# Down's blocks by block products in place of full-width products, and half of the weight sums by transfers

## The chip, the core and the metric

The kernel runs on one core of a Trainium2 chip. The metric is the device time of one execution in microseconds; a kernel's time is the median of its runs. All numbers of a profile come from one further execution, recorded by the hardware profiler.

## What is computed

The reference is one block of a diffusion transformer on 512 tokens of width 2048: a conditioning vector gives shifts, scales and gates, a token mixer of two branches is followed by a gated residual, and then comes the feed-forward part that this change is about, with an inner width D_FF of 5632:

```python
mod = jax.nn.silu(c) @ w_ada[layer] + b_ada[layer]
sh1, sc1, g1, sh2, sc2, g2 = jnp.split(mod[:, None, :], 6, axis=-1)
...
def swiglu(h, wg, wu, wd):
    return (jax.nn.silu(h @ wg) * (h @ wu)) @ wd
...
y, yc = token_mix(h, hc, p, need_ctx)
x = x + g1 * rmsnorm(y, norm_mix_post[layer])
h = modulate(x, norm_ffn_pre[layer], sh2, sc2)
x = x + g2 * rmsnorm(swiglu(h, w_gate[layer], w_up[layer], w_down[layer]), norm_ffn_post[layer])
```

Everything is float32. The kernel splits each operand into a high and a low part (hi, lo) that TensorE takes, and forms each product by three matmuls: hi x hi, hi x lo and lo x hi.

## The kernel before

Tokens stand on the free axis, features on the partitions, so that D_FF is 44 blocks of 128 rows and the width of 2048 is 16 blocks. A weight piece is 128 x 1024 numbers (512 KB, eight blocks of 128 x 128). SyncE's queue loads it (`raw`, or `rq` in the quads), ScalarE casts it to `whi`, VectorE subtracts to get `wlo`, and TensorE runs 24 matmuls on it. Both tiles have three buffers, so that weights are prepared some three pieces ahead of TensorE.

The feed-forward part has these stages:

- `gate_up` makes the first six of the 44 blocks of gate and up by halves of 256 tokens. `sums_of_x` meanwhile forms the sums of activation blocks that the next stage needs (`th`, `tl`; the plain blocks are `fh`, `fl`).
- `quad` treats the 38 remaining blocks as 19 pairs, for `w_gate` and then `w_up`: 38 quads. A quad is a product of 2 x 2 blocks of weights (two output blocks, two halves of the depth) with 2 x 2 blocks of activations (two halves of the depth, two halves of the tokens), formed by seven products of blocks instead of eight. Each product is one weight piece, 24 matmuls of 256 columns (`acc` in PSUM). Four weight pieces r11, r12, r21, r22 are loaded, and the sums of them that the seven products need are formed in place by four VectorE additions of 128 x 1024 (`rq<-rq,rq`). `early` and `end` combine the products into `R` on VectorE; gate times up goes to `hd` in DRAM.
- Down: `act_load` brings `hd` back (512 KB each), splits it, and `down_piece` runs ten chunks of four of the 44 blocks, at the full 512 columns, with sums kept in `y2`. Between its pieces come steps of the conditioning vector's product (`ada(1)`: a weight load and two VectorE operations of 128 x 512 each), the last of which give the final gate.
- The last chunk runs by two halves of 256 tokens (`down`), so that `last_done` and `finish` can normalise the first half, add the residual `x1d` and store while TensorE works on the second.

The order of each engine's instructions is set by a scheduler from the order of the code and by the buffers of each pool; `feed` and `push` put weights ahead of their matmuls.

## Time and profile before

| what | us |
|---|---|
| median of three runs | 2559.17 |
| lowest, highest | 2533.26, 2560.54 |
| the profiled execution, its time | 2562.26 |
| its span (first to last instruction) | 2560.4 |
| TensorE busy | 2436.5 (95%) |
| VectorE busy | 1802.5 (70%) |
| ScalarE busy | 914.5 (36%) |
| GpSimd busy | 458.5 (18%) |

PE is TensorE, PEld its weight load, DVE VectorE, ACT ScalarE, POOL GpSimd, SP SyncE, whose queue (SPq) issues the transfers. Matmuls overlap, so a matmul's duration (0.28 us at 256 columns) is longer than the distance to the next one; how fast TensorE goes is read from starts, or from the count in a window. "Idle before" is the time an engine stood still ahead of an instruction, with what ended it. Clock 1.00 is the full TensorE clock.

### The profile page before, as it was taken

What the parts mean: (1) busy time and instruction counts of PE and PEld (TensorE: products, weight loads), DVE (VectorE), ACT (ScalarE), POOL (GpSimd) and SP (SyncE); (2) the same over time, 40 slices, a digit from 0 to 9 for tenths busy, and PEclk for the clock granted to TensorE, in tenths of its full rate; (3) what the DMA queues carried; (4) which work ended last, traced back from release to release, by engine and by line L of the source; (5) the groups of instructions that cost most, each with busy time, mean ns of one, the idle gap of its engine ahead of it and who ended that gap; (6) DMA issues with size and microseconds to landing.
All of it is one profiled execution on the core that took longest, in us unless ns stands there. A gap on an engine that the chain in (4) does not pass through costs nothing.

```text
span 2560.4 us, 37510 instructions
## 1 busy us (share of the span) xinstructions
PE 2436.5 (95%) x14932; PEld 2118.2 (83%) x14932; DVE 1802.5 (70%) x2278; ACT 914.5 (36%) x1273; POOL 458.5 (18%) x421
## 2 busy tenths in 40 slices
PE   8999999899899999998999999999999899999996
PEld 3467879677667788998999999999999788888885
DVE  7986756788878867688877788878887763242234
ACT  3143325222223312355444444444444332231133
POOL 1230010566524244752000000000000000000004
PEclk9999999999899999999999999999999899999998
DMA  8867754435355565545633333333333484242233
GB/s 288 315 217 236 245 163 157 160 131 170 124 201 188 202 251 179 206 155 195 217 110 124 124 125 108 124 125 123 116 121 119 145 296 147 99 146 93 99 107 120
DMA packets 151223, 420.39 MB, mean 164 GB/s; under 512 B 15391, under 2 KB 46047, under 8 KB 149512
## 3 DMA queue, kind: packets, MB, share of 16 engines
q1 hardware_dynamic: 151048, 418.00, 48.0%
q8 instruction: 117, 1.92, 0.3%
q14 instruction: 58, 0.48, 0.1%
HBM read 382.82 MB, written 35.13 MB: 163 GB/s over the span
## 4 chain that ended last, share of the span: by engine, by line
PE 51%; DVE 2%; issue 1%; POOL 1%; DMA 1%; ACT 1%; POOLq 0%; SPq 0%; ACTq 0%; DVEq 0%
PE acc L83 22%; PE acc L1361 10%; PE acc L1360 10%; PE acc L1362 10%; POOL gs L80 1%; DVE wlo L80 1%; DMA x<-x1d 0%; DVE y2a L80 0%; ACT whi L170 0%; POOL y2a L80 0%; PE aux L83 0%; DMA raw<-in_w_down 0%; POOL yTa L80 0%; DMA st<-hd 0%; POOL r L80 0%
## 5 line engine op out<-in xcount | busy, mean ns | idle before, releaser
L80 DVE TENSOR_TENSOR wlo<-raw,whi 128x1024 fp32r<-128x1024 f32 x268 | 342.4, 1278 | 347.0 <-ACT whi L170 340.3
L170 ACT CAST whi<-raw 128x1024 fp32r<-128x1024 f32 (+1 forms) x284 | 293.2, 1033 | 740.1 <-PE acc L83 548.2
L80 DVE TENSOR_TENSOR wlo<-rq,whi 128x1024 fp32r<-128x1024 f32 x266 | 323.8, 1223 | 122.7 <-ACT whi L1321 117.9
L1321 ACT CAST whi<-rq 128x1024 fp32r<-128x1024 f32 x266 | 279.0, 1049 | 358.8 <-PE acc L1361 318.6
L1360 PE MATMUL acc<-th,whi 128*128 128x256 f32 x1216 | 341.7, 281 | 0.0
L1361 PE MATMUL acc<-tl,whi 128*128 128x256 f32 x1216 | 341.7, 281 | 0.0
L1362 PE MATMUL acc<-th,wlo 128*128 128x256 f32 x1216 | 341.7, 281 | 0.0
L80 POOL TENSOR_TENSOR gs<-gs,sq 128x256 f32<-128x256 f32 x91 | 84.8, 935 | 1386.4 <-ACT sq L74 1382.9
L83 PE MATMUL acc<-hh,whi 128*128 128x512 f32 x688 | 284.4, 415 | 4.4 <-ACT hh L74 4.2
L83 PE MATMUL acc<-hl,whi 128*128 128x512 f32 x688 | 276.8, 402 | 2.8 <-DVE hl L77 2.8
L83 PE MATMUL acc<-ah,whi 128*128 128x512 f32 (+1 forms) x688 | 264.0, 384 | 12.5 <-ACT ah L187 12.5
L83 PE MATMUL acc<-hh,wlo 128*128 128x512 f32 x688 | 275.9, 401 | 0.0
L83 PE MATMUL acc<-al,whi 128*128 128x512 f32 (+1 forms) x688 | 263.4, 383 | 0.0
L83 PE MATMUL acc<-ah,wlo 128*128 128x512 f32 (+1 forms) x688 | 263.3, 383 | 0.0
L1360 PE MATMUL acc<-fh,whi 128*128 128x256 f32 x912 | 256.3, 281 | 0.0
L1361 PE MATMUL acc<-fl,whi 128*128 128x256 f32 x912 | 256.3, 281 | 0.0
L1362 PE MATMUL acc<-fh,wlo 128*128 128x256 f32 x912 | 256.3, 281 | 0.0
L77 DVE SCALAR_TENSOR_TENSOR ada<-raw,cc,ada 128x512 f32<-128x512 f32 x240 | 202.8, 845 | 54.0 <-DMA raw<-in_ada 51.1
L1360 PEld LDWEIGHTS acc<-th,whi 128*128 128x128 f32 x1216 | 233.5, 192 | 0.0
L1361 PEld LDWEIGHTS acc<-tl,whi 128*128 128x128 f32 x1216 | 228.2, 188 | 0.0
L1362 PEld LDWEIGHTS acc<-th,wlo 128*128 128x128 f32 x1216 | 228.2, 188 | 0.0
L80 DVE TENSOR_TENSOR rq<-rq,rq 128x1024 f32<-128x1024 f32 x152 | 185.6, 1221 | 2.1
(325 smaller groups left out, 5001.6 us busy)
## 6 DMA issues: line engine op xcount, KB each, us to landing
raw<-in_ada SPq DMA_DIRECT2D x128, 512.0 KB, 3.9
raw<-in_w_down SPq DMA_DIRECT2D x88, 512.0 KB, 3.2
rq<-in_w_gate SPq DMA_DIRECT2D x76, 512.0 KB, 3.8
rq<-in_w_up SPq DMA_DIRECT2D x76, 512.0 KB, 3.4
ada<-in_ada SPq DMA_DIRECT2D x64, 512.0 KB, 4.9
raw<-in_w_hy SPq DMA_DIRECT2D x44, 512.0 KB, 4.0
raw<-in_w_out SPq DMA_DIRECT2D x41, 512.0 KB, 4.2
raw<-in_w_xbc SPq DMA_DIRECT2D x38, 512.0 KB, 3.8
```

The lines of the kernel that those rows point to most:

```text
L77: nc.vector.scalar_tensor_tensor(out=o, in0=a, scalar=s, in1=b, op0=op0, op1=op1)
L80: e.tensor_tensor(out=o, in0=a, in1=b, op=op)
L83: nc.tensor.matmul(o, lhsT, rhs, start=start, stop=stop)
L170: nc.scalar.copy(out=hi[:, :n], in_=raw[:, :n])
L1321: nc.scalar.copy(out=hi, in_=raw)
L1360: nc.tensor.matmul(p, wh, xh, start=k == 0, stop=False, skip_group_check=True)
L1361: nc.tensor.matmul(p, wh, xl, start=False, stop=False, skip_group_check=True)
L1362: nc.tensor.matmul(p, wl, xh, start=False, stop=k == 7, skip_group_check=True)
```

## The change

Sixteen of the 22 pairs of blocks of `hd` (pairs 3 to 18) now go through down by block products too: 16 more quads, in two chunks (c) of eight pairs, eight quads (m) each, on weights `w_ds`. Their activations are the results of the gate and up quads: `sums` forms the sums T when an up quad ends, and `hd` holds for each pair four result blocks and four sums. They take the place of the old activation operands in the same tiles: `replace` hangs 56 loads of 128 KB (`op_load`) and 56 splits (`op_split`: a ScalarE cast and a VectorE subtraction of 128 x 256) per chunk on the steps of the stream, around the quad at which the tile's old content has been used. Results of a down quad go to `y2d` in DRAM; at the end the first chunk's are loaded and the second chunk's added by accumulating transfers.

In every quad the sums of weights are formed in another way: a transfer issued by GpSimd adds the block of weights in DRAM to the piece in SBUF (`load_s1` for r21, and another into r11 after its first product); two additions remain on VectorE. The order of the seven products differs with it. Every third quad's first matmul is split at column 160. The steps `ada(1)` stand in the gate and up quads.

The six pairs left over (twelve blocks, `CP`) run in down by halves of 256 tokens, on weights `w_dc`, which are loaded once for each half; `kept` and `wload_big`, which kept weights for the second half, go.

```diff
-    hd = dram.tile([44, 128, 512], F32, name="hd")
+    hd = dram.tile([22, 128, 8, 256], F32, name="hd")
...
+    CP = [0, 1, 2, 19, 20, 21]
+    KICK = 160
...
+    def op_load(dst, src):
+        nc.sync.dma_start(dst[1].bitcast(F32), src)
+
+    def op_split(dst):
+        split(dst[0], dst[1], dst[1].bitcast(F32))
+
+    def replace(q, c, area):
+
+        for j in range(1, 7):
+            n = 7 * (q - 1) + j
+            for k in range(8):
+                d = place(j, k, 0)
+                at(n + 4, lambda d=d, k=k, j=j: op_load(d, hd[CH[c][k]][:, SRC[j], :]))
+                at(n + 6 + k // 4, lambda d=d: op_split(d))
+        for k in range(8):
+            d = place(0, k, area)
+            at(7 * (q - 4) + k, lambda d=d, k=k: op_load(d, hd[CH[c][k]][:, 0, :]))
+            at(7 * (q - 4) + k + 2, lambda d=d: op_split(d))
...
+    def load_s1(q):
+        r = qload("raw", quads[q][0][1, 0])
+        nc.gpsimd.dma_start(r, quads[q][0][1, 1], accum_op=ADD)
+        return r
...
-                    nc.tensor.matmul(p, wh, xh, start=k == 0, stop=False, skip_group_check=True)
+
+                    for c0, c1 in ((0, KICK), (KICK, 256)) if i == k == 0 and q % 3 == 0 else ((0, 256),):
+                        nc.tensor.matmul(p[:, c0:c1], wh, xh[:, c0:c1], start=k == 0 and c0 == 0, stop=False,
+                                         skip_group_check=True)
...
+                nc.sync.dma_start(hd[m][:, 0:4, :], R)
+                if m not in CP:
+                    sums(m, R)
+            else:
+                act(R[:, 1, :], R[:, 1, :], AF.Copy, scale=-1.0)
+                nc.sync.dma_start(y2d[kind, m], R)
+
+        def sums(m, R):
+            T = gu.tile([128, 4, 256], F32, tag="T", name=nm("T"))
+            tt(nc.vector, T[:, 0:4:2, :], R[:, 1:4:2, :], R[:, 0:2, :], SUB)
+            tt(nc.vector, T[:, 1, :], R[:, 3, :], T[:, 0, :], SUB)
+            tt(nc.vector, T[:, 3, :], T[:, 1, :], R[:, 2, :], SUB)
+            nc.sync.dma_start(hd[m][:, 4:8, :], T)
...
         feed(r11, body(0))
         feed(r12, body(1))
-        tt(nc.vector, r11, r11, r21, ADD)
-        feed(r11, body(2))
-        tt(nc.vector, r21, r21, r22, ADD)
+        feed(r22, body(2))
+        nc.gpsimd.dma_start(r11, src[1, 0], accum_op=ADD)
         feed(r21, body(3))
-        if nxt:
-            nxt.append(qload("ra", I[nxt[1]][2 * nxt[0], 0]))
-        tt(nc.vector, r11, r11, r22, ADD)
+        if more:
+            nxt["r11"] = qload("ra", quads[q + 1][0][0, 0])
         feed(r11, body(4))
-        if nxt:
-            nxt.append(qload("ra", I[nxt[1]][2 * nxt[0], 1]))
+        if more:
+            nxt["r21"] = load_s1(q + 1)
+        tt(nc.vector, r22, r22, r11, ADD)
         feed(r22, body(5))
-        tt(nc.vector, r11, r11, r12, ADD)
-        feed(r11, body(6))
...
+        if more:
+            nxt["r12"] = qload("ra", quads[q + 1][0][0, 1])
+        tt(nc.vector, r12, r12, r22, ADD)
+        if q < NG:
+            ada(1)
+        feed(r12, body(6))
+
+    replace(NG, 0, 256)
+    replace(NG + 8, 1, 0)
...
+    y2t = [gu.tile([128, 4, 256], F32, tag=f"th{m}", name=f"y2{m}") for m in range(8)]
+    for m in range(8):
+        nc.sync.dma_start(y2t[m], y2d[0, m])
+        nc.gpsimd.dma_start(y2t[m], y2d[1, m], accum_op=ADD)
...
+    def down(q, i, h, ps, done):
+        def run(w):
+            for u in range(8):
+                s, k = divmod(i * 8 + u, 12)
+                if k == 0:
+                    ps[s] = acc()[:, 0:256]
...
     for h in range(2):
         done = last_done(h)
         for q in range(8):
-            if not h and q > 2:
-                kept[q] = wload_big(I["w_down"][NCHUNK - 1, q], q - 3)
-            kept[q] = down(NCHUNK - 1, q, h * 256, h * 256 + 256, done, kept[q])
+            ps = {}
+            for i in range(3):
+                down(q, i, h, ps, done)
```

On VectorE in the middle of the gate and up quads, the sequence of one quad before (`rq` are weight pieces: r11 is rq_14985, r12 rq_15017, r21 rq_15078, r22 rq_15080):

```order
L80 TENSOR_TENSOR wlo_15083<-rq_14985,whi_15082 128x1024
L80 TENSOR_TENSOR R_14853<-R_14853,acc_14992 128x2x256
L80 TENSOR_TENSOR rq_14985<-rq_14985,rq_15078 128x1024
L80 TENSOR_TENSOR wlo_15118<-rq_15017,whi_15117 128x1024
L80 TENSOR_TENSOR R_14853<-R_14853,acc_14931 128x256
L80 TENSOR_TENSOR rq_15078<-rq_15078,rq_15080 128x1024
L80 TENSOR_TENSOR R_14853<-R_14853,acc_15092 128x512
L80 TENSOR_TENSOR wlo_15147<-rq_14985,whi_15146 128x1024
L80 TENSOR_TENSOR rq_14985<-rq_14985,rq_15080 128x1024
L80 TENSOR_TENSOR wlo_15181<-rq_15078,whi_15180 128x1024
L80 TENSOR_TENSOR wlo_15212<-rq_14985,whi_15211 128x1024
L80 TENSOR_TENSOR rq_14985<-rq_14985,rq_15017 128x1024
```

and after (r11 is rq_15124, r12 rq_15188, r22 rq_15224, r21 rq_15155; the accumulating transfer into rq_15124 lies between its subtraction and the addition that reads it):

```order
L80 TENSOR_TENSOR wlo_15227<-rq_15124,whi_15226 128x1024
L80 TENSOR_TENSOR R_14989<-acc_15230,R_14989 128x256
L80 TENSOR_TENSOR R_14989<-R_14989,acc_15163 128x256
L80 TENSOR_TENSOR wlo_15256<-rq_15188,whi_15255 128x1024
L80 TENSOR_TENSOR R_14989<-R_14989,acc_15163 128x2x256
L80 TENSOR_TENSOR R_14989<-R_14989,acc_15130 128x512
L80 TENSOR_TENSOR wlo_15290<-rq_15224,whi_15289 128x1024
L80 TENSOR_TENSOR R_14989<-R_14989,acc_15069 128x256
L80 TENSOR_TENSOR rq_15224<-rq_15224,rq_15124 128x1024
L80 TENSOR_TENSOR rq_15188<-rq_15188,rq_15224 128x1024
L80 TENSOR_TENSOR wlo_15324<-rq_15155,whi_15323 128x1024
L80 TENSOR_TENSOR wlo_15354<-rq_15124,whi_15353 128x1024
```

The four additions have become two, which stand together ahead of the subtractions of r21 and of the second use of r11.

On VectorE where down begins, before (`al<-st,ah` splits the reloaded `hd`):

```order
L77 SCALAR_TENSOR_TENSOR ada_7630<-raw_19469,cc,ada_7630 128x512
L80 TENSOR_TENSOR wlo_19476<-raw_19473,whi_19475 128x1024
L77 SCALAR_TENSOR_TENSOR ada_7630<-raw_19469,cc,ada_7630 128x512
L77 SCALAR_TENSOR_TENSOR ada_7630<-raw_19525,cc,ada_7630 128x512 x2
L80 TENSOR_TENSOR al_19404<-st_19401,ah_19403 128x512
L80 TENSOR_TENSOR al_19408<-st_19401,ah_19407 128x512
L80 TENSOR_TENSOR al_19414<-st_19411,ah_19413 128x512
L80 TENSOR_TENSOR al_19418<-st_19411,ah_19417 128x512
L80 TENSOR_TENSOR al_19428<-st_19425,ah_19427 128x512
```

and after, in the quad ahead of the first down quad (`fl<-fl,fh` and `tl<-tl,th` are the subtractions of `op_split`):

```order
L80 TENSOR_TENSOR rq_21275<-rq_21275,rq_21179 128x1024
L80 TENSOR_TENSOR fl_8868<-fl_8868,fh_8867 128x256
L80 TENSOR_TENSOR rq_21243<-rq_21243,rq_21275 128x1024
L80 TENSOR_TENSOR wlo_21375<-rq_21210,whi_21374 128x1024
L80 TENSOR_TENSOR fl_8897<-fl_8897,fh_8896 128x256
L80 TENSOR_TENSOR fl_8915<-fl_8915,fh_8914 128x256
L80 TENSOR_TENSOR fl_8944<-fl_8944,fh_8943 128x256
L80 TENSOR_TENSOR wlo_21405<-rq_21179,whi_21404 128x1024
L80 TENSOR_TENSOR fl_9058<-fl_9058,fh_9057 128x256
L80 TENSOR_TENSOR fl_9064<-fl_9064,fh_9063 128x256
L80 TENSOR_TENSOR fl_9070<-fl_9070,fh_9069 128x256
L80 TENSOR_TENSOR fl_9076<-fl_9076,fh_9075 128x256
```

The splits of the reloaded activations now stand in groups of three to five between the weight subtractions of a running quad.

On SyncE's queue where the block products end, before (the end of gate and up):

```order
L162 DMA raw_19473<-in_w_down 128x1024
L1392 DMA hd<-R_19100 128x2x512
L162 DMA raw_19525<-in_ada 128x1024
L162 DMA raw_19529<-in_w_down 128x1024
L1451 DMA st_19401<-hd 128x2x512
L1451 DMA st_19411<-hd 128x2x512
L1451 DMA st_19425<-hd 128x2x512
L162 DMA raw_19579<-in_ada 128x1024
L1451 DMA st_19435<-hd 128x2x512
L1451 DMA st_19449<-hd 128x2x512
```

and after (the end of down's block products; `tl<-hd` are operands of the last twelve blocks, `y_<-y2d` the first chunk's results):

```order
L1352 DMA tl_10354<-hd 128x256 x2
L1352 DMA tl_10412<-hd 128x256 x2
L1352 DMA tl_10123<-hd 128x256
L1531 DMA y_23520<-y2d 128x1024
L1531 DMA y_23521<-y2d 128x1024
L1531 DMA y_23522<-y2d 128x1024
L1531 DMA y_23523<-y2d 128x1024
L1444 DMA y2d<-R_23221 128x1024
L1531 DMA y_23524<-y2d 128x1024
L1531 DMA y_23525<-y2d 128x1024
L1531 DMA y_23526<-y2d 128x1024
L1531 DMA y_23527<-y2d 128x1024
```

The reload of all of `hd` has given way to eight loads of `y2d` that stand among the weight pieces.

## Rows read from the trace of the kernel before

**Rows 1.** The page: busy time by engine; the granted clock by slice.

```profile
PE 2436.5 (95%) x14932; PEld 2118.2 (83%) x14932; DVE 1802.5 (70%) x2278; ACT 914.5 (36%) x1273; POOL 458.5 (18%) x421
...
PEclk9999999999899999999999999999999899999998
```

**Rows 2.** Windows: busy time and count by engine, clock, DMA share, GB/s.

```profile
1300.00:2000.00 700.00, 700.00 (x5946) 700.00 (x5945) 564.57 (x620) 303.63 (x373) 0.00 (x0) 1.00 0.36 120
2044.00:2048.00 4.00, 3.50 (x8) 2.49 (x9) 2.66 (x5) 2.82 (x6) 0.00 (x0) 0.50 0.95 355
2100.00:2400.00 300.00, 300.00 (x1333) 248.63 (x1332) 97.11 (x101) 75.46 (x87) 0.00 (x0) 1.00 0.36 123
2486.00:2499.00 13.00, 13.00 (x111) 13.00 (x110) 9.96 (x18) 11.37 (x26) 5.46 (x7) 1.00 0.24 88
2536.00:2561.00 25.00, 1.94 (x9) 1.13 (x8) 8.72 (x13) 1.33 (x4) 6.13 (x5) 0.52 0.43 136
```

**Rows 3.** One matmul's line: count, duration ns, first and last start.

```profile
L1360 PE MATMUL acc<-fh,whi x912: 281/281/281, 1280.0 to 2031.5; 128*128 128x256 f32 x183
```

**Rows 4.** Timeline from gate and up to down: start, duration, engine, operation, idle before.

```profile
2031.76 0.28 PE L1362 MATMUL acc<-fh,wlo 128*128 128x256 f32 x1
...
2039.06 1.41 SPq L1451 DMA_DIRECT2D st<-hd  x3
...
2044.50 0.79 PE L83 MATMUL acc<-ah,whi 128*128 128x512 f32 x1 [12.46 <-ACT ah L187]
...
2048.77 0.39 PE L83 MATMUL acc<-ah,whi 128*128 128x512 f32 x1
```

**Rows 5.** Timeline of TensorE around a hitch at 1243 us.

```profile
1240.49 0.28 PE L83 MATMUL acc<-fh,whi 128*128 128x256 f32 x1
...
1242.98 0.28 PE L83 MATMUL acc<-fl,whi 128*128 128x256 f32 x1
1243.14 0.39 PE L83 MATMUL acc<-fh,wlo 128*128 128x256 f32 x1
1243.36 0.28 PE L83 MATMUL acc<-fh,whi 128*128 128x256 f32 x1
```

**Rows 6.** Windows of two stretches with 256-column matmuls.

```profile
1140.00:1152.00 12.00, 12.00 (x108) 12.00 (x108) 10.86 (x17) 6.41 (x11) 8.19 (x8) 1.00 0.61 198
1180.00:1228.00 48.00, 48.00 (x410) 48.00 (x409) 46.05 (x74) 28.47 (x40) 0.00 (x0) 1.00 0.55 194
```

**Rows 7.** Groups by form from 1290 to 2030 us: busy, mean; idle before.

```profile
L80 DVE TENSOR_TENSOR wlo<-rq,whi 128x1024 fp32r<-128x1024 f32 x261 | 317.7, 1223 | 118.7 <-ACT whi L1321 113.9
L1321 ACT CAST whi<-rq 128x1024 fp32r<-128x1024 f32 x260 | 272.7, 1049 | 348.6 <-PE acc L1361 315.0 <-issue 28.6 <-DVE rq L80 5.0
...
L80 DVE TENSOR_TENSOR R<-R,acc 128x512 f32<-128x512 f32 x75 | 51.1, 681 | 0.0
L80 DVE TENSOR_TENSOR R<-R,acc 128x256 f32<-128x256 f32 x75 | 31.3, 418 | 1.3
```

**Rows 8.** Timeline of VectorE: operations back to back.

```profile
1519.05 0.42 DVE L80 TENSOR_TENSOR R<-R,R 128x256 f32<-128x256 f32 x1
1519.39 0.42 DVE L77 SCALAR_TENSOR_TENSOR R<-R,R 128x256 f32<-128x256 f32 x1
```

**Rows 9.** Transfers: count, KB each, median us from issue to landing.

```profile
rq<-in_w_gate SPq DMA_DIRECT2D x76, 512.0 KB, 3.8
rq<-in_w_up SPq DMA_DIRECT2D x76, 512.0 KB, 3.4
...
hd<-sg SPq DMA_DIRECT2D x12, 128.0 KB, 3.1
```

**Rows 10.** GpSimd's additions: the page's group; the tile's from 2400 us (min/median/max).

```profile
L80 POOL TENSOR_TENSOR gs<-gs,sq 128x256 f32<-128x256 f32 x91 | 84.8, 935 | 1386.4 <-ACT sq L74 1382.9
...
L80 POOL TENSOR_TENSOR gs<-gs,sq x26: 723/740/1195, 2489.5 to 2534.4; 128x256 f32<-128x256 f32 x26
```

**Rows 11.** The chain that ended last: start, us, what.

```profile
2545.47 4.14 DMA x<-x1d
```

More of the change, by code (lines that the diff above doesn't have):

```diff
@@ L1342, in qload, with quad @@
         return raw
+    def load_s1(q):
+        r = qload("raw", quads[q][0][1, 0])
+        nc.gpsimd.dma_start(r, quads[q][0][1, 1], accum_op=ADD)
+        return r
+    y2d = dram.tile([2, 8, 128, 4, 256], F32, name="y2d")
     gate = {}
-    def quad(j, mat, r11, r12, nxt):
-        src, m1, m2 = I[mat], 2 * j, 2 * j + 1
+    nxt = {"r11": qload("ra", quads[0][0][0, 0]), "r12": qload("ra", quads[0][0][0, 1]), "r21": load_s1(0)}
+    def quad(q):
+        src, area, kind, m = quads[q]
         ps = {}
@@ L1396, in quad @@
+        def sums(m, R):
[4 more added lines that the diff above has]
+            nc.sync.dma_start(hd[m][:, 4:8, :], T)
+        r11, r12, r21 = nxt["r11"], nxt["r12"], nxt["r21"]
+        more = q + 1 < len(quads)
+        r22 = qload("raw", src[1, 1])
         feed(r11, body(0))
@@ L1408, in quad @@
+        tt(nc.vector, r22, r22, r11, ADD)
         feed(r22, body(5))
-        tt(nc.vector, r11, r11, r12, ADD)
-        feed(r11, body(6))
-    todo = [list(q) for q in quads()]
-    todo[0] += [qload("ra", I[todo[0][1]][2 * todo[0][0], i]) for i in range(2)]
-    for n, q in enumerate(todo):
-        quad(*q, todo[n + 1] if n + 1 < len(todo) else None)
+        if more:
[3 more added lines that the diff above has]
+            ada(1)
@@ new lines, in quad, with last_ops @@
+        feed(r12, body(6))
+    replace(NG, 0, 256)
+    replace(NG + 8, 1, 0)
+    yo = {}
+    def last_ops():
+        lf = 7 * len(quads)
+        blocks = [(j, b) for j in CP for b in range(2)]
+        y = {}
+        for i, (j, b) in enumerate(blocks):
+            if i < 8:
+                y[i, 0] = place(0, i, 256)
+                n = 7 * (NG + 9) + 3 * i
+            else:
+                y[i, 0] = [tx[0][1][:, i - 8, :], tx[1][1][:, i - 8, :]]
+                n = lf - 7 + 5 + 4
+            at(n, lambda i=i, j=j, b=b: op_load(y[i, 0], hd[j][:, 2 * b, :]))
+            at(n + 2, lambda i=i: op_split(y[i, 0]))
+            y[i, 1] = [tx[2 + i // 4][1][:, i % 4, :], tx[5 + i // 4][1][:, i % 4, :]]
+        return y
@@ L1416, in block_kernel, with rest @@
+    yo = last_ops()
+    for q in range(len(quads)):
+        quad(q)
     while pend:
         pend.pop()()
-    first = [wload(I["w_down"][0, 0])]
-    for op in late:
-        op()
-    late.clear()
+    first = [wload(I["w_dc"][0, i]) for i in range(1)]
+    def rest():
+        for op in late:
+            op()
+        late.clear()
+        for fn in hooks.pop(step[0], ()):
+            fn()
+        step[0] += 1
+    rest()
     w, fn = ahead.pop(0)
     fn(w)
-    first.append(wload(I["w_down"][1, 0]))
@@ L1425, in block_kernel @@
-    for op in late:
-        op()
-    late.clear()
+    first.append(wload(I["w_dc"][0, 1]))
+    rest()
     w, fn = ahead.pop(0)
     fn(w)
-    for op in late:
-        op()
-    late.clear()
+    rest()
+    while hooks:
+        rest()
     stash.extend(first)
-    gu_cm.__exit__(None, None, None)
-    fd_cm = pool("fd")
-    fd = fd_cm.__enter__()
-    fd.tile([128, 16], F32, name="pad3")
-    y2_cm = pool("y2", side="right")
-    y2p = y2_cm.__enter__()
-    y2a = y2p.tile([128, 16, 512], F32, name="y2a")
@@ L1463, in down_piece @@
-    def down_piece(c, q, ps, first, last, done):
-        def run(wt):
-            for s in range(2):
-                if first:
-                    ps.append(acc())
-                for k in range(4):
-                    ah, al = acts[c * 4 + k]
-                    mm3(ps[s], *wt[s * 4 + k], ah, al, first and k == 0, last and k == 3)
-                if last:
-                    done(q * 2 + s, ps[s])
-            pump()
-        push(I["w_down"][c, q], run)
-    def early_loads(i0, i1):
-        for i in range(i0, i1, 2):
-            act_load(i)
-            yield
```

157 lines of the change are left out of this document (69 added, 88 removed).

## The prediction

> **What bounds the kernel now.** I began with the page's busy shares and its slices, to see whether one engine sets the pace throughout: TensorE is busy 95% of 2560.4 us, VectorE 70%, and the granted clock is at 0.9 or more of full in all but a handful of slices [rows 1]. Then I cut the span into stages by windows, since the change touches only what comes after 1280 us. From 1300 to 2000 us, the gate and up projections by block products, TensorE is busy all 700 us at full clock, VectorE 564.57 us, ScalarE 303.63 us, GpSimd nothing, and the transfers fill 0.36 of the DMA engines [rows 2]. So TensorE alone bounds the stage, and an edit is worth what it takes from or adds to TensorE's instruction stream, plus any wait that reaches it.
>
> The line view dates the stage: matmuls of the line that stands first in each group of three run from 1280.0 to 2031.5 us [rows 3]. All 6384 matmuls (38 quads x 7 products x 8 blocks x 3) fit in 751.9 us, 117.8 ns each, without one stall. Down runs its full-width part at 300 us for 1331 whole matmuls of 512 columns, 225.4 ns each [rows 2] (a window's count holds about two matmuls cut by its edges; I take these off). Its last chunk, in halves of 256 tokens, takes 13 us for 109, 119 ns [rows 2].
>
> Two stretches are not TensorE's. Between gate/up and down, TensorE stops at 2031.76 and resumes at 2044.50: down's first operands must come back from DRAM (issued at 2039.06) [rows 4]. And from 2536 us TensorE is done but for nine small matmuls; some 24 us of normalisation, residual loads and stores end the program [rows 2].
>
> **One thing decides a good part of the sum: the spacing of a 256-column matmul takes levels.** The same form runs at 113.2 ns (22 steps from 1240.49 to 1242.98) before a hitch at 1243.14 us, and slower behind it; at 113.2 ns again in the window from 1140 (12 us for 106), and at 117.7 ns in the one from 1180 (48 us for 407.7) [rows 5, 6]. The clock is at full in both windows. A level holds until something breaks the stream, and the block-product stage drew the slow one at its start and kept it for 752 us, having no break. Had it drawn the fast one, 6384 x 4.5 ns = 29 us would be missing; the runs before differ by 26 to 27 us (2533.26 against 2559.17 and 2560.54), which fits one draw for the whole stage. The change splits the first matmul of every third quad into 160 + 96 columns: a break each time.
>
> **The change, part by part.** I build the span from 1280.0 us, since all before it is untouched.
>
> *Matmuls.* After the change 6384 (gate, up) + 16 x 168 = 2688 (down by block products) + 48 pieces x 24 = 1152 (down by halves) = 10224 matmuls of 256 columns remain. At 117.8 ns they take 1204 us, at 113.2 ns 1157 us. With a new draw at each split and three of five fast (of some dozen stretches between breaks before 1250 us about that share was fast; [rows 5, 6] show one stretch of each kind and a hitch between two), the mean is 115.1 ns: **1176.8 us**. The 22 splits add a matmul each, at most 0.11 us: **2.5 us**. For comparison, the old down took 2536 - 2032 = 504 us, junction included; 3840 matmuls at 115.1 ns are 442.
>
> *The junction* of 12.7 us, and the nine 512-column matmuls at half clock behind it (4.27 us from the first to the tenth instead of 2.03, some 2 us [rows 4]), go: the down quads follow the up quads in one stream.
>
> *Operands replaced in place.* What hid the old reload was idle VectorE; now it sits in the stream. For each of two chunks, 56 blocks of 128 x 256 are reloaded, cast by ScalarE and subtracted by VectorE, 48 of them within about nine products around quads 38 and 46, since a buffer can only be overwritten when the previous quad has used it. VectorE then has, by its rows, 51 small subtractions (0.42 us each, 0.34 from one start to the next, as 1519.05 to 1519.39: 17.3), ten weight subtractions (1.22, and 1.15 with the same overlap: 11.5), two adds (2.3) and R operations at 0.68 and less (3.9): 35 us [rows 7, 8]. TensorE's nine products take 24.9. Less a lead of some 2 us (ScalarE's casts wait for TensorE to free a buffer, 315 us of such waits, so weights are three blocks ahead [rows 7]), VectorE is late by about 8 us, twice: **16 us**. ScalarE has 51 x 0.37 + 10 x 1.05 = 29 us, SyncE 51 issues; both lie beside it. From below, 8 us in all if the sums leave room; from above 30, if loads of 3.1 us each [rows 9] wait in turn for buffers.
>
> *Weight sums.* VectorE loses two of four adds per quad (2.3 us of 19.6); it was no bound, so nothing is gained. SyncE and GpSimd get, per quad, six transfers of 512 KB instead of four: DMA share 0.36 x 1.5 = 0.54, still room. But a wait is added. r11 is used by product 0, then GpSimd's queue sends the accumulating transfer into it, and VectorE's r22 += r11 waits for its landing; queued behind that add on VectorE are r12 += r22 and the weight subtractions of products 3 and 4, which TensorE needs. Call A the time from the end of product 0's subtraction to the landing. From the moment the three-deep weight buffers free, five products (14.1 us) pass until product 3 must start; a cast (1.05), product 0's subtraction, two adds and product 3's subtraction (4 x 1.15) must fit: A may be 14.1 - 1.05 - 4.6 = 8.4 us without TensorE noticing. No transfer of before is an accumulating one, nor issued by GpSimd. The nearest rows are the plain 512 KB loads at 3.4 and 3.8 us, and, for a second read of the old contents on the same engines, twice that, 7.6 [rows 9]. I take 6.5 (nearer to the upper, since r21's accumulating transfer is ahead of it on GpSimd's queue and the engines are fuller): cost **0**, hidden by products 1 and 2. If the cover goes, each us over 8.4 costs 1 us in each of 53 quads.
>
> A row on what GpSimd does beside VectorE: its 128 x 256 additions have a median of 740 ns in the last 160 us, where VectorE is idle much of the time, but a mean of 935 over the program [rows 10]. The Trainium skill, "SBUF — State Buffer", section "Who interferes with whom", says that a VectorE instruction with two SBUF inputs holds up GpSimd instructions that read SBUF, and in "SBUF: two separate sides" that a GpSimd-issued transfer can be starved while its descriptors can't be written. The trace agrees on the first as far as [rows 10] go; no run here shows the second. [...]
>
> *The end of the block products.* Eight loads of 512 KB (y2d, 4 MB) stand on SyncE's queue ahead of the fourth piece of the remaining weights, and eight accumulating ones follow on GpSimd's; the best rate in these rows is 355 GB/s [rows 2], so the loads take 12 us, while TensorE has about 8 us of pieces in hand. With the first addition waiting for its accumulation: **8 us** (3 to 20). Small stalls elsewhere: **3 us**. *Tail*: the same chain of residual loads and stores, one of its loads alone 4.14 us [rows 11]: **24 us** as before. The sums T of the up quads (some 2 us of VectorE in each of 16) and the modulation's steps, moved from down into the quads, lie in VectorE's free 20%.
>
> **Sum.** 1280.0 + 1176.8 + 2.5 + 16 + 8 + 3 + 24 = 2510.3 us of span; the execution was 1.9 us longer than its span (2562.26 against 2560.4): 2512 us. The profiled execution stands 3 us above the median of the runs, 2559.17, and shares its slow level. What a measurement of this kernel can tell from no change is about 1%, 25.6 us, so "faster" means under 2534.
>
> **Rivals.**
> 1. *The accumulating transfers are late* and VectorE's add stops the stream; this ends on the other side. Place: r22 += r11 in every quad. Price: 53 us per us by which A exceeds 8.4; break-even with 2562 at A = 9.35. At A = 10 it is 2512 + 85 = 2597. For: no such transfer in the trace, two reads, GpSimd's queue, engines half full. Against: the plain rows at 3.4 to 3.8 leave over twice their time. Chance 0.22, most of it between 2560 and 2640.
> 2. *The split doesn't do what it is there for* and the stream keeps 117.8 ns: + 27 us, 2539. For: the halves near the end ran 119 ns after breaks. Against: [rows 5] show a change at a hitch of some 0.05 us. 0.17.
> 3. *Every draw is fast*: 113.2 ns throughout, -19 us, 2493. For: the fastest run before. 0.10.
> 4. *The two replacements and the junction cost twice* what I gave (VectorE becomes the bound for longer): + 24 us, 2536. 0.06.
>
> **How the numbers follow.** The forecast, 2495 to 2530 by the bounds of its terms, has 0.45. The range, 2486 to 2580, takes in all but the late part of rival 1 and the extreme of rival 3. Faster by over 1%: the forecast, rival 3, and the share of rival 2 with smaller other terms, 0.60. Within 1%: most of rivals 2 and 4 and the mild part of 1, 0.22. Slower: 0.18.
>
> **What would show it.** In the changed kernel's profile: TensorE starting at 1280 and without idle time until quad 38; the spacing changing at the split matmuls, in windows of three quads (504 matmuls, about 57 or 59 us); two stretches, near 2010 and 2175 us, where TensorE waits for VectorE's subtractions with operand subtractions ahead of them; the accumulating transfers landing within 8 us. TensorE waiting for the weight subtractions 3 or 4 in every quad, behind an add that waits for a transfer, would prove me wrong; so would a junction of 20 us or more before the halves.

## The result, and the profile after

The changed kernel takes 2658.57 us (median of four runs, 2651.55 to 2662.24) against 2546.22 us before (2528.13 to 2560.54, four runs): ratio 1.0442, interval 1.0353 to 1.053. The four runs of before fall into two groups, 2528 and 2533 us, and 2559 and 2561, and the median lies between them. The changed kernel is slower by 4.4%, outside the range of 2486 to 2580 that was given. The profiled execution took 2660.69 us, with a span of 2658.9.

The first view is the page of the changed kernel: busy time by engine, the granted clock and the DMA share by slice, the queues, and the chain that ended last.

```profile
PE 2432.1 (91%) x16490; PEld 2179.3 (82%) x16490; DVE 1905.7 (72%) x2505; ACT 1008.8 (38%) x1464; POOL 565.4 (21%) x537
...
PEclk9999999899999999999999989999999999999798
DMA  8866744454357666456666666666676786876965
...
q1 hardware_dynamic: 171432, 457.86, 51.3%
q0 software_dynamic: 16704, 60.82, 12.8%
...
PE 24%; DMA 18%; DVE 9%; issue 4%; ACT 2%; POOL 1%; SPq 0%; POOLq 0%; DVEq 0%; ACTq 0%
```

The engine that had 95% [rows 1] has 91%, over a span that is 98.5 us longer, and its clock falls below 0.9 of full in places. DMA engines that were a third busy in the block products are at six to eight tenths. A queue stands there that before did not have: q0, software_dynamic, GpSimd's transfers. It moved 60.82 MB in 12.8% of the engines' time, q1 457.86 MB in 51.3%: per percent, q0 moved 4.75 MB and q1 8.92. And the chain that ended last has DMA for 18% of the span. So TensorE no longer sets the pace alone; transfers do in part.

Windows say where. These are the changed kernel's, with busy time and count by engine, the clock, the DMA share and GB/s:

```profile
1300.00:2000.00 700.00, 632.01 (x5184) 626.19 (x5182) 470.62 (x573) 263.92 (x333) 55.37 (x62) 0.95 0.65 178
2483.00:2506.00 23.00, 0.43 (x2) 0.43 (x2) 1.19 (x3) 2.79 (x5) 5.15 (x6) 0.55 1.06 274
```

Where before 5946 matmuls fitted in 700 us without a gap [rows 2], 5184 do now, though they are, when they run, closer together (113 to 118 ns). Cut finer, for TensorE alone:

```profile
1300.00:1700.00 400.00, 351.23 (x2838) 0.93 0.65 179
1800.00:2000.00 200.00, 190.49 (x1612) 0.97 0.66 174
```

A quad has 168 matmuls (168.33 with the splits), so that the counts, less the two cut by the edges, give 23.7 us a quad up to 1700 us and 20.9 from 1800, where 113.3 ns would give 19.1. The view of waits from 1290 to 2000 us (who waited for what, us, times, longest) names the place:

```profile
POOL rq L1383 <- DMA rq<-in_w_gate: 165.5, 8, 22.8
...
DVE rq L80 <- DMA rq<-in_w_up: 67.9, 16, 6.4
...
PE acc L1409 <- DVE wlo L80: 62.4, 24, 5.4
DVE rq L80 <- DMA rq<-in_w_gate: 45.0, 13, 7.0
DVE ada L77 <- DMA raw<-in_ada: 24.8, 12, 3.6
...
POOL rq L1460 <- DVE wlo L80: 4.1, 4, 1.4
```

TensorE waits for a weight subtraction (24 times, up to 5.4 us), VectorE for an addition of weights that waits for a transfer (29 times, up to 7.0), and GpSimd's queue, which has nothing else to do in a quad, stands nearly always at L1383, r21's transfer: L1460, r11's, is among the waits four times only, for 1.4 us at most, since else it is found ready when its turn comes. One case in the timeline (start, duration, engine, operation, idle before), from the quad that starts at 1518 us and the end of the one ahead of it, with TensorE's window behind its wait as the last line (busy time and count, clock, DMA share, GB/s):

```profile
1512.58 0.75 DVE L77 SCALAR_TENSOR_TENSOR ada<-raw,cc,ada 128x512 f32<-128x512 f32 x1
1513.24 2.36 DVE L80 TENSOR_TENSOR wlo<-rq,whi 128x1024 fp32r<-128x1024 f32 x2
...
1513.36 1.47 SPq L1378 DMA_DIRECT2D rq<-in_w_up  x2
...
1519.78 0.88 POOL L1383 DMA_DIRECT2D rq<-in_w_up  x1 [22.44 <-ACT R L1423]
...
1520.41 1.17 POOL L1460 DMA_DIRECT2D rq<-in_w_gate  x1
...
1528.98 1.23 DVE L80 TENSOR_TENSOR rq<-rq,rq 128x1024 f32<-128x1024 f32 x1 [6.98 <-DMA rq<-in_w_gate]
...
1532.00 0.58 PE L1409 MATMUL acc<-th,wlo 128*128 128x256 f32 x1 [5.38 <-DVE wlo L80]
1532.38 0.41 PE L1406 MATMUL acc<-th,whi 128*128 128x256 f32 x1
...
1532.00:1536.00 4.00, 4.00 (x18) 0.50 0.67 172
```

Read it from the subtraction of r11, the second of the two at 1513.24, done at 1515.60. From then on GpSimd could send the transfer that adds to r11 (L1460). But the one ahead of it on the queue, r21's of the next quad (L1383), goes out at 1519.78 only, and r11's behind it at 1520.41. What r21's waited for is its plain load, issued at 1513.36, when a step of the conditioning vector (1512.58) had freed a buffer, and landed 5.7 us later. r11's transfer lands at 1528.9, 8.5 us later. VectorE, whose next operation is r22 += r11 (1528.98), has stood for 6.98 us with two weight subtractions behind it, and TensorE stands 5.38 us at its product 3. A is thus 13.3 us here: 4.8 of waiting in the queue and 8.5 of transfer. It is the longest of the 54 quads. Reckoned from the trace in the same way, A is 10.9 us at the median in quads 0 to 20 (6.9 to 13.3, above 8.4 in 18 of 21; the wait ahead of the issue is 2.6 at the median) and 8.3 in quads 21 to 36 (above 8.4 in 7 of 16).

The wait is not all that is lost. Behind it the granted clock is 0.50, the lower of the two levels (1.2 GHz), and matmuls follow at 0.21 us instead of 0.113. By the starts of the matmuls in quads 0 to 20, TensorE's 31 stands add 68 us to the pace of 113.3 ns, and 260 matmuls at about half pace add another 26.

The end of the block products, in the chain that ended last:

```profile
2482.71 0.13 PE acc L1561
...
2485.72 24.35 DMA raw<-in_w_dc
2510.15 1.06 ACT whi L170
2511.23 1.24 DVE wlo L80
```

A weight piece of 512 KB issued at 2485.72 takes 24.35 us to land, behind eight loads of y2d and with their accumulating transfers in flight (DMA share 1.06 from 2483 to 2506 us); TensorE stands 22.7 us.

### The profile page after: what moved, and what is told of

Its sections match the earlier page's. It is cut to its first block, busy times and chain, and to the rows that moved or that the text cites. A ratio compares the mean times of both kernels' runs of the same rounds, so it can differ in the third digit from the quotient of the medians.

```text
span 2658.9 us, 42037 instructions
## 1 busy us (share of the span) xinstructions
PE 2432.1 (91%) x16490; PEld 2179.3 (82%) x16490; DVE 1905.7 (72%) x2505; ACT 1008.8 (38%) x1464; POOL 565.4 (21%) x537
## 3 DMA queue, kind: packets, MB, share of 16 engines
q1 hardware_dynamic: 171432, 457.86, 51.3%
q0 software_dynamic: 16704, 60.82, 12.8%
## 4 chain that ended last, share of the span: by engine, by line
PE 24%; DMA 18%; DVE 9%; issue 4%; ACT 2%; POOL 1%; SPq 0%; POOLq 0%; DVEq 0%; ACTq 0%
PE acc L1409 6%; DMA rq<-in_w_gate 6%; DMA rq<-in_w_up 6%; PE acc L1406 6%; PE acc L1408 6%; DVE wlo L80 4%; PE acc L83 3%; DMA rq<-in_w_ds 3%; PE acc L1561 1%; PE acc L1558 1%; PE acc L1560 1%; DVE rq L80 1%; DMA raw<-in_w_dc 1%; DMA fl<-hd 1%; ACT whi L1335 1%
## 5 line engine op out<-in xcount | busy, mean ns | idle before, releaser
L1335 ACT CAST whi<-rq 128x1024 fp32r<-128x1024 f32 x378 | 397.1, 1051 | 636.7 <-PE acc L1408 447.5
L1409 PE MATMUL acc<-th,wlo 128*128 128x256 f32 x1728 | 501.8, 290 | 84.4 <-DVE wlo L80 84.0
L80 DVE TENSOR_TENSOR wlo<-rq,whi 128x1024 fp32r<-128x1024 f32 x378 | 457.1, 1222 | 122.5 <-ACT whi L1335 114.0
L1406 PE MATMUL acc<-th,whi 128*128 128x256 f32 x1728 | 496.3, 287 | 2.8 <-ACT whi L1335 2.8
L1408 PE MATMUL acc<-tl,whi 128*128 128x256 f32 x1728 | 495.0, 286 | 0.0
L1406 PE MATMUL acc<-fh,whi 128*128 128x256 f32 (+2 forms) x1314 | 360.2, 276 | 3.8 <-ACT whi L1335 2.0
L1406 PEld LDWEIGHTS acc<-fh,whi 128*128 128x128 f32 x1314 | 245.7, 188 | 4.4 <-ACT whi L1335 2.2
L1408 PEld LDWEIGHTS acc<-fl,whi 128*128 128x128 f32 x1296 | 243.7, 188 | 0.0
L1409 PEld LDWEIGHTS acc<-fh,wlo 128*128 128x128 f32 x1296 | 243.7, 188 | 0.0
L83 PEld LDWEIGHTS acc<-hh,whi 128*128 128x128 f32 x688 | 133.8, 195 | 39.5 <-issue 5.9
```

Of the source, the lines that this page charges most:

```text
L80: e.tensor_tensor(out=o, in0=a, in1=b, op=op)
L83: nc.tensor.matmul(o, lhsT, rhs, start=start, stop=stop)
L1335: nc.scalar.copy(out=hi, in_=raw)
L1406: nc.tensor.matmul(p[:, c0:c1], wh, xh[:, c0:c1], start=k == 0 and c0 == 0, stop=False, skip_group_check=True)
L1408: nc.tensor.matmul(p, wh, xl, start=False, stop=False, skip_group_check=True)
L1409: nc.tensor.matmul(p, wl, xh, start=False, stop=k == 7, skip_group_check=True)
```

## The experiments

Two theories of the loss stood at the outset: Q, that r11's transfer is late because of its place on GpSimd's queue, behind r21's of the next quad, which in turn waits for r21's plain load and that for a buffer; and T, that an accumulating transfer is too long by itself. A third, V, was that VectorE has too much to do. Us per quad below are read from windows as above, or from the first matmuls of the quads in the trace where quads are named by number (0 to 37 gate and up, 38 to 53 down; 0 to 20 hold steps of the conditioning vector).

**All sums on VectorE (e1).** In the changed kernel:

```diff
     def load_s1(q):
-        r = qload("raw", quads[q][0][1, 0])
-        nc.gpsimd.dma_start(r, quads[q][0][1, 1], accum_op=ADD)
-        return r
+        return qload("raw", quads[q][0][1, 0])
...
-        nc.gpsimd.dma_start(r11, src[1, 0], accum_op=ADD)
+        tt(nc.vector, r11, r11, r21, ADD)
+        tt(nc.vector, r21, r21, r22, ADD)
```

> All four sums of weights are formed by VectorE again (r21 and r22 are loaded plain, r11 += r21, r21 += r22, then the two that were there); the rest of the change stays. Theory Q (the transfers' place on GpSimd's queue) and theory T (the accumulating transfer itself takes too long) both expect the waits ahead of product 3 to go: quads 0 to 20 at 19.2 to 19.9 us each instead of 23.8, the whole at about 2535 us (2515 to 2560). Theory V (VectorE has too much to do in a quad, the steps of the conditioning vector among it) expects the quads to stay above 22 us and the whole at or above 2650.

Measured: 2523.49 us (2513.99 to 2531.01, ten runs), ratio to before 0.9958 (0.9941 to 0.9975). 135 us less than the changed kernel, by this edit alone. TensorE's windows:

```profile
1300.00:1700.00 400.00, 397.46 (x3500) 1.00 0.50 165
1800.00:2000.00 200.00, 200.00 (x1767) 1.00 0.43 137
```

19.25 us a quad up to 1700 us, 19.07 from 1800: no wait is left but 2 us in three quads. V is out, since VectorE has two additions more in each quad.

**r21's sum on VectorE, r11's a transfer (e2).** As e1, but `tt(nc.vector, r21, r21, r22, ADD)` stands beside the transfer into r11, which stays.

> Only r21's sum goes back to VectorE (r21 += r22), r11's stays an accumulating transfer, so nothing of another quad is ahead of it on GpSimd's queue and no second accumulating transfer is in flight. Q: the transfer is issued at once when product 0's subtraction ends and lands some 5.5 us later, the smallest seen; under 8.4 us, so quads 0 to 20 take 19.2 to 20 us and the whole about 2545 (2525 to 2565). T: it still takes 7.6 to 8.5 us from issue, the wait stays at 0 to 2 us a quad, quads 0 to 20 at 20 to 22 us and the whole 2575 to 2610.

Measured: 2567.54 us (2563.92 to 2575.07), ratio 1.0133 (1.0108 to 1.0157), between the ranges of the two theories. The time from issue to landing of r11's transfer, in the changed kernel (L1460) and here (L1458), min, median and max:

```profile
DMA to landing us min/median/max: 5.3/7.6/9.1
```

```profile
DMA to landing us min/median/max: 5.1/5.4/8.0
```

Alone, the transfer takes 5.4 us instead of 7.6. Quads from 1800 us on are at 19.23, as Q says. Up to 1700 us they are at 21.0, as T says, but the timeline shows another reason:

```profile
1420.49 0.75 DVE L77 SCALAR_TENSOR_TENSOR ada<-raw,cc,ada 128x512 f32<-128x512 f32 x1 [0.54 <-DMA raw<-in_ada]
1421.16 1.22 DVE L80 TENSOR_TENSOR wlo<-rq,whi 128x1024 fp32r<-128x1024 f32 x1
...
1422.40 0.33 SPq L1378 DMA_DIRECT2D rq<-in_w_up  x1
...
1427.86 1.23 DVE L80 TENSOR_TENSOR rq<-rq,rq 128x1024 f32<-128x1024 f32 x1 [3.35 <-DMA rq<-in_w_gate]
```

The addition that waits 3.35 us at 1427.86 is r21 += r22 of the next quad (the order of VectorE's instructions has it ahead of the next quad's first subtraction), and the load that lands as it starts is the one issued at 1422.40 (5.4 us to landing; the tensor named in the bracket is inferred, and not the right one here). That load could go out only when the subtraction at 1421.16 had freed a buffer: of the three, one held a step's weights and one r21, and the subtraction itself stood behind the step at 1420.49. So the steps, whose weights share the three buffers of r21 and r22, are a likely part of it (e11 tests it), and neither theory had them as a cause for VectorE.

**The steps' weights in tiles of their own (e5).** 

```diff
-                    raw = wraw(I["ada2"][sec - 1, g, pc])
+                    halves = [rsm.tile([128, 512], F32, tag="mt", bufs=2, name=nm("mta")) for _ in range(2)]
```

> Both accumulating transfers stay. The conditioning vector's weights (the 21 steps that fall in quads 0 to 20) are loaded into two tiles of 128 x 512 of their own instead of a buffer of the three that r21 and r22 use. Q: r21's plain load no longer waits for VectorE's step to free a buffer, so r21's transfer no longer stands waiting ahead of r11's: quads 0 to 20 come down from 23.8 us to those of quads 21 to 37, 20.5, the whole to about 2590 (2570 to 2610). T: the buffer has nothing to do with it, quads 0 to 20 stay above 23 us, the whole at 2640 to 2660.

Measured: 2623.97 us (2618.54 to 2627.95), 35 us less than the changed kernel, half of what Q expected and in the range of neither theory. Quads 0 to 20 took 21.8 us on average, 21 to 36 still 20.7.

**r21's transfer held back (e10).** 

```diff
-    def load_s1(q):
+    def load_s1(q, after=None):
         r = qload("raw", quads[q][0][1, 0])
+        if after is not None:
+            z = gu.tile([128, 1], F32, tag="z", bufs=2, name=nm("z"))
+            nc.gpsimd.tensor_scalar(out=z, in0=after[:, 0:1], scalar1=0.0, scalar2=None, op0=MUL)
+            tt(nc.gpsimd, r[:, 0:1], r[:, 0:1], z, ADD)
...
-            nxt["r21"] = load_s1(q + 1)
+            nxt["r21"] = load_s1(q + 1, r11)
```

> Everything of the change stays, both accumulating transfers too; only r21's transfer of the next quad is held back until r11's of this quad has landed (GpSimd multiplies one column of r11 by zero and adds it to r21's first column, 128 x 1 each, ahead of the issue). Q: r11's transfer is then issued as soon as product 0's subtraction ends and lands alone in about 5.4 us, under the 8.4: quads 0 to 20 at 19.3 to 20.3 us instead of 23.8, quads 21 to 36 at 19.3 instead of 20.5, the whole at about 2545 us (2530 to 2565). T: two transfers are too much in whichever order; quads 0 to 20 stay above 22 us, the whole above 2620.

Measured: 2592.94 us (2580.35 to 2596.11), ratio 1.0199 (1.0141 to 1.0257), 66 us less than the changed kernel; this too lies between the two theories.

```profile
1300.00:1700.00 400.00, 369.87 (x3119) 0.98 0.71 194
1800.00:2000.00 200.00, 200.00 (x1766) 1.00 0.70 190
```

From 1800 us on: 19.09 us a quad, as e1, with both transfers in place. That part of the loss was the order. (The edit takes away two things at once, the wait in the queue and the two transfers' running side by side: r11's lands after 5.5 us at the median in quads 21 to 36, where it took 7.45 in the changed kernel. Which of them counts for how much was not separated.) Up to 1700 us 21.6 us are left. A is no longer the reason, since it is above 8.4 in none of quads 0 to 36 by more than 0.02 us. The timeline shows VectorE standing for a step's weights:

```profile
1572.57 0.33 SPq L162 DMA_DIRECT2D raw<-in_ada  x1
...
1579.07 0.49 DVE L326 TENSOR_SCALAR ada<-raw,cc 128x512 f32<-128x512 f32 x1 [4.89 <-DMA raw<-in_ada]
1579.47 1.22 DVE L80 TENSOR_TENSOR wlo<-rq,whi 128x1024 fp32r<-128x1024 f32 x1
```

The load is issued at 1572.57, when one of the three buffers comes free; the step has its place on VectorE's queue ahead of a weight subtraction (1579.47), and VectorE stands 4.89 us. From 1290 us to the last step, VectorE's waits for the steps' weights (us, times, longest) are these in e10 and in e1, which has the same steps and buffers:

```profile
DVE ada L77 <- DMA raw<-in_ada: 60.6, 19, 5.3
```

```profile
DVE ada L77 <- DMA raw<-in_ada: 12.1, 9, 1.7
```

In the changed kernel it was 24.8 (above). With the wait for r11 mended, the wait for the steps grew.

**The steps moved (e11).** The kernel of e10, with `if 14 <= q < NG` ahead of `ada(1)`.

> The kernel with r21's transfer held back (e10), and the 21 steps of the conditioning vector moved from quads 0 to 20 to quads 14 to 34. If these steps are the second cause (VectorE waits in line for a step's weights, which got a buffer of the three late), the loss moves with them: quads 0 to 13 at 19.0 to 19.8 us each, quads 14 to 34 at about 22, the whole unchanged at 2580 to 2600. If the early quads are slow for another reason (what runs before them, the stores of T), quads 0 to 13 stay at 21.5 or more and quads 21 to 34 at 19.2.

One run: 2597.31 us. TensorE's windows ahead of the steps, and among them:

```profile
1300.00:1530.00 230.00, 230.00 (x2031) 1.00 0.72 195
1560.00:1960.00 400.00, 366.61 (x3087) 0.97 0.70 193
```

19.08 us a quad without the steps, 21.8 with them. The loss went where they went.

**All three hindrances away, the transfers kept (e13).** The edits of e10, e5 and e4 (below) together.

> Both accumulating transfers kept, with all three hindrances taken away at once: r21's transfer held back (e10), the conditioning vector's weights in tiles of their own (e5), the loads of y2d spread (e4). If these three are the whole loss, quads 0 to 36 at 19.1 to 19.8 us and the whole at 2515 to 2530, level with the kernel of e7. If the transfers cost something of their own beside them, quads 0 to 20 above 20.5 and the whole above 2545.

Measured: 2557.80 us (2545.91 to 2568.12, ten runs), ratio 1.0013 (0.9975 to 1.0052). The ratio is to runs of before of which 8 of 13 were in the upper of two groups (2560 to 2567; the lower 2530 to 2542); to a before at 2535, as beside e1 and e7, it would be 1.009. 101 us less than the changed kernel, but 36 more than e7, its counterpart with the sums on VectorE. Quads 21 to 36 are at 19.08 us; quads 0 to 20 at 20.7 where e7's are at 19.4 (27 us in all), and quads 45 to 47 take 75.9 us against 65.5. So the numbers are those of the second outcome. But the edit did not take the steps' wait away, as this line from 1290 to 1790 us shows:

```profile
DVE ada L77 <- DMA mta<-in_ada: 30.3, 17, 3.6
```

In tiles of their own the steps' weights still come late, more so than in e1, while A is above 8.4 us in quads 0 to 20 in the first quad alone. Behind the second replacement it is r11's transfer: 11.9 us from issue to landing in quad 47. What makes the steps' loads late here, the fuller DMA engines or the two small tiles, was not separated, so that a cost of the transfers' own is not shown for quads 0 to 20.

**The loads of y2d spread (e4).** 

```diff
-    for m in range(8):
-        nc.sync.dma_start(y2t[m], y2d[0, m])
-        nc.gpsimd.dma_start(y2t[m], y2d[1, m], accum_op=ADD)
+    y2_load(0)
...
                 down(q, i, h, ps, done)
+                if not h and i == 0 and q < 7:
+                    y2_load(q + 1)
```

> The eight loads of y2d and their accumulating transfers are issued one pair at a time between the weight pieces of the last stage, instead of all ahead of the fourth piece. If the 22.7 us wait of TensorE at 2483 us is the weight piece queued behind 4 MB on SyncE's queue, that wait shrinks to under 5 us and the whole comes to about 2640 (2632 to 2648); if it is the operands of the last blocks or the additions that are late, 2655 to 2662.

Measured: 2646.58 us (2645.42 to 2653.43), 12 us less. The longest wait of TensorE from 2470 us on came down from 22.7 to 5.0 us; some shorter ones came in its place. Whether the plain loads or the accumulating transfers made the larger part of the 22.7 was not separated.

**e1 and e4 together (e7).**

> All four weight sums on VectorE and the loads of y2d spread over the last stage (the two edits that helped, together). If their gains add: 2523 less 12, 2511 us (2505 to 2518). If the wait at the end of the block products has another cause once the stream is faster: 2518 to 2525.

Measured: 2521.46 us (2513.21 to 2524.16, ten runs), ratio to before 0.9919 (0.9883 to 0.9955): the fastest kernel of this study, and ahead of before. The gains did not add: 2 us less than e1, not 12. The two profiles have the last stage 9 us shorter, from the first matmul behind the quads to the end (186.2 to 176.7), but e7's has quads 21 to 23 and 47 to 50 at the slow spacing (19.8 us each instead of 19.0), which e1's has nowhere, and the first replacement 2 us longer (29.4 against 27.4).

**No split (e8).** The kernel of e7, with no matmul split.

> The kernel of e7 with no matmul split at column 160. If the level of the 256-column spacing is drawn at a break and kept, some executions hold the slow level for the 38 quads ahead of the first operand replacement or longer: these at 2535 to 2550 us, the others at about 2508, and the profile shows one level per stretch. If the splits do nothing: all executions at 2508 to 2516, no second group, and the share of fast spacings in the profile as with the splits.

Measured: 2533.74 us (2517.87 to 2540.02, ten runs), ratio 0.9968 (0.9933 to 1.0003). The profiled execution was the fastest of the ten. Two windows of it, the second within quads 39 to 45, between the two operand replacements:

```profile
1800.00:1900.00 100.00, 100.00 (x884) 1.00 0.46 145
2060.00:2160.00 100.00, 100.00 (x852) 1.00 0.42 133
```

113.4 ns in the first, 117.6 in the second, and every quad from 39 to 45 took 19.8 us: one level held from break to break. The nine slower runs have no trace, so that the level of their quads is inferred; none came near the 2508 expected of the others. With splits ten runs lie between 2513 and 2524; without, nine of ten between 2528 and 2540. The splits are worth some 12 us here.

**The split alone, on the kernel before (e9).** `(0, 160), (160, 256)` for the first matmul of every third of the 38 quads.

> The kernel before with only the split of every third quad's first matmul (13 splits). If a split sets the level: no execution above 2545, the group at 2555 to 2564 is gone, median 2530 (2526 to 2535). If it does nothing: two groups as in the runs of before, about one execution in four to two near 2560.

Measured: 2536.70 us (2533.91 to 2538.12, twelve runs), ratio 0.9985 (0.9954 to 1.0015). Beside it the kernel before had 29 runs: 24 from 2529.07 to 2543.18, and five from 2559.03 to 2568.08. None is in the upper group, and the median is that of before's lower group (2535.10), a little above the 2526 to 2535 expected. Were the share still five of 29, twelve runs without one would come about once in ten times. The profile adds to it: over the 700 us that had 5946 matmuls [rows 2]:

```profile
1300.00:2000.00 700.00, 700.00 (x6179) 1.00 0.37 122
```

That is 113.3 ns, in all 38 quads.

**Half of the replacement's subtractions on GpSimd (e12).** On e7: `tt(nc.gpsimd if turn[0] % 2 else nc.vector, ...)` in `op_split`.

> The kernel of e7 (sums on VectorE, loads of y2d spread), with every second subtraction of the operand replacement on GpSimd instead of VectorE (128 x 256; some 0.8 to 0.95 us there). If VectorE's work is what makes quads 38 and 46 long (29.4 and 26.6 us against 19.1), taking 24 to 28 of 0.34 us each from it takes 8 us off the first and 7 off the second: about 21 us each, the whole at 2508 (2502 to 2515). If the loads or ScalarE's casts are the bound there, or GpSimd and VectorE hold each other up, quads 38 and 46 stay within 3 us and the whole at 2517 to 2525.

Measured: 2524.96 us (2523.99 to 2528.27), 3.5 more than e7. In e7 VectorE is busy throughout the first replacement, first fence; the second has e12 in the same stretch:

```profile
2015.00:2035.00 20.00, 13.80 (x112) 13.02 (x111) 20.00 (x39) 15.42 (x39) 0.00 (x0) 1.00 0.84 274
```

```profile
2015.00:2035.00 20.00, 14.14 (x105) 13.58 (x103) 20.00 (x26) 13.15 (x33) 13.40 (x14) 0.91 0.59 190
```

VectorE is full in both, but gets through 39 instructions in e7 and 26 in e12. The same subtraction, by form, around the first replacement of e7 and of e12:

```profile
L80 DVE TENSOR_TENSOR wlo<-rq,whi 128x1024 fp32r<-128x1024 f32 x15 | 18.1, 1214 | 2.5 <-ACT whi L1335 2.5
...
L80 DVE TENSOR_TENSOR tl<-tl,th 128x256 fp32r<-128x256 f32 x32 | 11.4, 410 | 0.0
```

```profile
L80 DVE TENSOR_TENSOR wlo<-rq,whi 128x1024 fp32r<-128x1024 f32 x15 | 20.0, 1336 | 0.3 <-ACT whi L1335 0.3
...
L80 POOL TENSOR_TENSOR tl<-tl,th 128x256 fp32r<-128x256 f32 x16 | 16.7, 1072 | 7.1 <-ACT th L1359 7.1
...
L80 DVE TENSOR_TENSOR tl<-tl,th 128x256 fp32r<-128x256 f32 x16 | 11.3, 752 | 0.0
```

410 ns become 752 beside GpSimd, whose own take 1072. Quads 37, 38, 45 and 46 together take 105.1 us, against 95.6 in e7. VectorE, full throughout, is the bound of the replacement, as the first theory of this experiment says; taking work off it failed because VectorE's own instructions last longer beside the helper's.

## Why the prediction was wrong

The sum went by the span: 2510.3 forecast, 2658.9 measured. By the first matmuls of the quads, the terms are:

| stretch | forecast | measured |
|---|---|---|
| up to the first quad | 1280.0 | 1283.5 |
| quads 0 to 20 | 406.9 | 499.1 |
| quads 21 to 36 | 310.0 | 327.7 |
| quads 37 to 53 (with 16 for the replacements) | 345.4 | 364.2 |
| from there to the end (132.6 of matmuls, 8, 3 and 24) | 167.6 | 184.5 |

(The forecast has 19.37 us for a quad of 168.33 matmuls at 115.1 ns.)

*The step that failed* is the value of A: "I take 6.5 ... cost 0, hidden by products 1 and 2". The limit of 8.4 us, the instruction that would wait (r22 += r11), what is queued behind it and the place where TensorE would stand (product 3) were as described under rival 1, which is the case that came about, at 2658.57 beyond the part of it that the range took in. A was 10.9 us at the median of quads 0 to 20 and 13.3 in the quad shown. What I bounded was a transfer's duration, and that bound was not far off: 5.4 us alone, 7.6 at the median behind another. What I left out was the time before the issue. I had noted that r21's transfer is ahead of r11's on GpSimd's queue, and had put it into the choice within the range, but did not ask what that one waits for. It waits for its plain load, and the load for a buffer. At rival 1's price the excess of A over 8.4 in all 54 quads comes to 67 us; e10, which mends the order, gives back 66, and its quads 21 to 36 come to 19.2 us with both transfers in place. The price itself left out the clock: the matmuls at half pace behind the stands are 26 us of quads 0 to 20.

*A second step failed beside it*: that the conditioning vector's steps "lie in VectorE's free 20%". In VectorE's time they do; e1 has them too, and keeps 19.25 us. But each takes one of the three buffers of r21 and r22, so that a load waits for VectorE and VectorE for a load. The two together cost 92 us in quads 0 to 20: e10 leaves 57 of them, and e11 shows that these, some 2.7 us a quad, move with the steps. It takes both, the steps and the transfers: with the steps alone (e1) nothing is lost, and with the transfers alone (e10, quads 21 to 36) 2 us in 16 quads. The buffers are part of it (e5), and late loads another, since the wait stays in e13. The DMA share, put at 0.54, was 0.70 at full pace (e10 from 1800 us), where e1 has 0.43.

*The end of the block products* was a term of the right mechanism and the wrong size: 8 us (3 to 20) forecast, 22.7 measured. I set 12 us of loads against 8 of pieces in hand, and left the accumulating transfers' 4 MB as a small addition, though they run on the same engines at the same time: DMA share 1.06 (the share of each in the 22.7 was not separated).

*What held.* The operand replacement: 16 us forecast for two; in e1, where nothing else disturbs it, quads 38 and 46 take 27.4 and 26.6 us against 19.1 of their neighbours, 15.8 together, with VectorE busy throughout the first (28.0 of 28 us from 2002). The junction of 12.7 us is gone: the first down quad follows in the stream. The levels of the spacing: a split can end a slow stretch (e7: quads 21 to 23 slow, fast from the split of quad 24 on), though not each does (quad 21 was split too). One reading was off: behind the hitch at 1243.14 us [rows 5] the trace is back at 113.3 ns after four matmuls, and the slow level starts behind a break of 0.28 us at 1245.87. (The window from 1180 holds 408 matmuls less its edges, not 407.7: 117.6 ns.) The fast level was more frequent than the three in five that I used (of the spacings between 105 and 125 ns in the quads, 75% in the changed kernel and over 99% in e1).

*The base.* The execution profiled before is one with the slow level in all 38 quads. Of the runs of before, 24 of the 29 beside e9 and 13 of the 15 beside e1 are in the lower group, about 2535 us, but only 5 of the 13 beside e12 and e13: the share changes from one set of runs to the next. The forecast of 2512 was worked out from the trace, so that it does not hang on this; but the gain that it promised was against the upper group. With the sums back on VectorE, as in e1, the change comes to 0.996 of before's time.

Where the block products' gain went, then: 135 us to two sums by transfers (e1) in a stream with the conditioning steps, and 12 to loads issued all at once (e4), of which only 2 came back on top of e1 (e7). What is left, 14 us from 2535.51 to 2521.46, is half of what one level of spacing makes.

## What to carry to other kernels

When an edit puts a transfer between two operations, its price is from the moment that it could be issued to its landing: look up what stands ahead of it on the queue that issues it, what that waits for, and which buffers the loads behind that share, before taking a duration from a row. An engine with a free fifth can still be late if work is queued on it in order behind something that waits for a buffer. And before an edit is weighed against one profiled execution, see whether the runs fall into groups, and which of them the profile belongs to.

## What the runs showed of the hardware that was not expected

An accumulating transfer of 512 KB from DRAM into SBUF took 5.1 us at least and 5.4 at the median from issue to landing when alone (e2), where plain ones took 3.4 to 3.8 in the kernel before [rows 9]; in e2 itself, with its fuller engines, plain loads of weights took 4.0 to 5.0 at the median. In the changed kernel from 1960 to 2130 us the queues moved:

```profile
q1 hardware_dynamic: 9827, 24.29, 42.9%
q0 software_dynamic: 2304, 8.39, 27.7%
```

That is 8.39 MB in 27.7% of 16 engines' 170 us, 11.1 GB/s for an engine, against 24.29 MB in 42.9%, 20.8 GB/s, for the plain queue. The Trainium skill, "Collectives: The Full Stack", section "The bandwidth ceiling: the fold count and why AG ≠ RS ≠ AR", says of ReduceScatter that it runs at half of AllGather's rate because its addition needs two source reads. The trace agrees on the half, with 11.1 against 20.8; the reason no run here shows. Of starved descriptors, which the prediction names, e2 shows no sign: r11's transfer is issued 0.3 to 0.4 us after its subtraction and lands in 5.4 us at the median, beside a VectorE that is busy for 76% of the span.

VectorE's subtractions of 128 x 256 with both inputs in SBUF go from 410 to 752 ns, and those of weights of 128 x 1024 from 1214 to 1336, when GpSimd runs subtractions of its own beside them (e12). The Trainium skill, "SBUF — State Buffer", section "Who interferes with whom", says that such a VectorE instruction contends with a GpSimd instruction that reads SBUF; the trace agrees.

In these traces a stream of 256-column matmuls at full clock keeps one of two spacings, 113.3 or 117.8 ns, until something breaks it, and a matmul issued in two parts of 160 and 96 columns can be enough of a break. On the kernel before, none of twelve runs with such splits was in the group at 2559 to 2568 us, where five of 29 without were.
